# TensorE in program order for the first gate and up block of the feed-forward net

## The chip, the cores and the metric

The kernel runs on one core of a Trainium2 chip. The metric is the device time of one execution in microseconds; the kernel before takes 871.7 us (median of 3 runs, 871.03 to 872.21). Engines are named PE (TensorE, the matrix unit), DVE (VectorE), ACT (ScalarE), POOL (GpSimd) and SP (SyncE, which here issues nearly all DMAs). Each engine has its own queue of instructions and works it off in order; engines wait for one another through semaphores.

## What is computed

One layer of a decoder trunk for 512 tokens of width 1024 (float32): an input projection, sliding-window attention and gated linear attention side by side, a gated merge, a SwiGLU feed-forward net, a per-layer embedding gate and a last norm. The change touches the start of the feed-forward net:

```python
h = rms_norm(x, norm_ffn)
g, u = jnp.split(h @ w_ffn_in, 2, axis=-1)      # 1024 -> 2 x 2816
x = x + (jax.nn.silu(g) * u) @ w_ffn_out
```

## The kernel before

Matrix products in float32 accuracy are made of three products of split operands (`mm3`, L122 to L124): each operand is a high part (a copy, ACT, L111) and a low part (a subtraction, DVE, L112).

A gate or up block of 256 columns (`quad_pair`, L544) is computed by a Strassen-like scheme with seven products of quarter blocks instead of eight. In the names, fg00 is the first gate block, fu00 the first up block, fg01 the next gate block. Each block has four weight units (.0 to .3) and three PSUM banks (pa, pb, pc). One of the seven products is 12 matmuls (4 steps of `mm3`) of 128x256. In program order a block is: pa from unit .0; pb from .0; pa again from .1, accumulated on top; pc from .1; pa from .2; pb (other half) from .2; pa from .3. Since pa is a running sum, ACT copies it out after each of its products (`copy`, L580: fg00u twice, then fg00v, then g), and DVE adds such a copy to pb or pc (L576). The next product into pa may only start when the copy of the last has been made. The copies land in tiles of a pool with 8 buffers ("t2").

Ahead of the block stands the norm of x. Its rows are transposed, and the quarter blocks and the four Strassen sums of the activations are made by ACT and DVE (`column`, L1144; the names h2t, h_b, h_t). Between the transposes PE multiplies p by W_ple (pl0, pl1). ACT copies those results out (L1235, pl00o to pl13o, in t2 tiles too), and `aside` stores them to DRAM (L311) on SP's queue, behind the weight load issued last.

The order on each engine is made by a scheduler that goes by its own estimate of times, except inside a `manual_schedule` block, where the engines listed keep the order in which the code is written. In the kernel before, ACT, DVE and POOL keep the written order from behind the first up block on (L1306); PE is placed by the scheduler throughout the feed-forward net. For fg00 and fu00 the scheduler places all four engines.

Of the kernel before, what the change touches and what calls it, by code (L numbers as in the profile page):

```python
# [33 lines left out]
def hybrid_layer(  # L34
# [26 lines left out]
    nc = tc.nc  # L61
# [24 lines left out]
    def t2(name, shape=(P, 512), dt=F32):  # L86
        return tp.tile(list(shape), dt, tag="t2", name=name)
# [20 lines left out]
    def split(dst, src, scale=None, eng=nc.vector):  # L108
        hi, lo = dst
        if scale is None:  # L110
            ins = nc.scalar.copy(hi, src)  # L111
            eng.tensor_tensor(out=lo, in0=src, in1=hi.bitcast(F32), op=ALU.subtract)  # L112
        else:
            ins = nc.scalar.activation(hi, src, AF.Copy, scale=scale)  # L114
            nc.vector.scalar_tensor_tensor(  # L115
                out=lo, in0=src, scalar=scale, in1=hi.bitcast(F32), op0=ALU.mult, op1=ALU.subtract
            )
        return ins.ins
# [398 lines left out]
    def tok_inner(name, lhs, k0, nk, ncol, evac, per=2):  # L517

        nu = nk // per
        pss = [bank(f"{name}ps{t}") for t in range(NT)]  # L520
        for u in range(nu):
            w = W.take(f"{name}{u}")
            for t in range(NT):
                tok_mms(pss[t], w, lhs, t, k0 + per * u, per, ncol, u == 0, u == nu - 1)
                if u == nu - 1:
                    evac(t, pss[t])
                if t % 2:
                    yield
# [20 lines left out]
    def flush(late, every=False):  # L549

        for job in late or []:
            job[0] -= 1
        while late and (every or min(late)[0] < 1):
            late.pop(late.index(min(late)))[2]()
# [72 lines left out]
    def drive(stream, other=None, rate=1):  # L627
        for _ in stream:
            if other is not None:
                for _ in range(rate):  # L630
                    next(other, None)
# [533 lines left out]
    def xrow(t):  # L1165
        return xr[t // 2][:, t % 2, :]
# [84 lines left out]
    def x_half(i):  # L1251
        for t in (0, 1, 2, 3):
            ps = bank(f"xt{i}{t}")
            for j in range(4):
                nc.tensor.transpose(out=ps[:, tok(j)], in_=xrow(t)[:, tok(4 * i + j)], identity=ident)
            split(xT.part(i, ALL, tok(t)), ps.rearrange("p (j t) -> p j t", j=4))
            ss = sm.tile([P, 1], F32, tag="s2", name=f"x{i}{t}s")
            nc.scalar.activation(junk, xrow(t)[:, 512 * i : 512 * i + 512], AF.Square, accum_out=ss)
            if i == 0:
                part[t] = cpool.tile([P, 1], F32, name=f"x3{t}")  # L1260
                nc.vector.tensor_scalar(out=part[t], in0=ss, scalar1=4.0 / D, scalar2=4.0 * EPS, op0=ALU.mult, op1=ALU.add)
            else:
                m = add_mean(ss, D / 4, part[t], f"x{i}{t}m")
                r3[t] = cpool.tile([P, 1], F32, name=f"r3{t}")
                nc.gpsimd.tensor_tensor(out=r3[t], in0=m, in1=mhalf, op=ALU.pow)
            yield

    for gi, (f0, nf) in enumerate(FFN):
        act = Split(f"act{gi}", nf)

        def inner():
            for i in range(nf // 2):
                gs = [t2(f"g{gi}{i}{e}") for e in range(2)]
                us = []

                def silu(e, gs=gs):
                    yield [1, next(jobs), lambda: nc.scalar.activation(gs[e], gs[e], AF.Silu)]

                def mult(e, i=i, gs=gs, us=us):
                    yield [  # L1280
                        1 + e,
                        next(jobs),
                        lambda: nc.vector.tensor_tensor(out=us[e], in0=us[e], in1=gs[e], op=ALU.mult),  # L1283
                    ]
                    yield [3, next(jobs), lambda: split(act.rows(2 * i + e), us[e])]

                yield from quad_pair(f"fg{gi}{i}", h2.hT, gs, silu, late)
                us += [t2(f"u{gi}{i}{e}") for e in range(2)]
                yield from quad_pair(f"fu{gi}{i}", h2.hT, us, mult, late)

        def add_x2(i):
            def evac(t, ps):
                dst = xrow(t)[:, 512 * i : 512 * i + 512]
                nc.vector.tensor_tensor(out=dst, in0=ps, in1=dst, op=ALU.add)

            return evac

        stream, late, jobs = inner(), [], count()
        if gi == 0:
            for _ in range(8):  # L1300
                next(stream)

            W.after, W.SUMS = None, 4
            in_turn = tc.manual_schedule(engines={nc.scalar.engine, nc.vector.engine, nc.gpsimd.engine})
            in_turn.__enter__()
        drive(stream)  # L1306
        flush(late, True)
        drive(tok_inner(f"fo{gi}0", act, 0, nf, 512, add_x2(0)))
        last_half = tok_inner(f"fo{gi}1", act, 0, nf, 512, add_x2(1))
        if gi < len(FFN) - 1:  # L1310
            drive(last_half)
        else:
            in_turn.__exit__(None, None, None)
            drive(last_half, x_half(0), 1)
# [101 lines left out]
```

## Time and profile before

| | |
|---|---|
| median of 3 runs | 871.7 us |
| profiled execution, own time | 872.2 us |
| its span, first to last instruction | 870.4 us |
| PE busy | 854.0 us, 98% |
| DVE busy | 565.7 us, 65% |
| ACT busy | 446.2 us, 51% |
| POOL busy | 160.8 us, 18% |
| mean granted PE clock | 0.998 |

The span is the time between the first and the last instruction on the chip; the execution's own time is 1.8 us longer. Busy times are shares of the span and overlap between engines. A matmul's record is longer than its share of a stream, since matmuls are pipelined: the pace is read from start to start. Line numbers (L580) are those of the kernel before. In a timeline, a bracket at the end of a row gives the engine's idle time ahead of it and what ended it.

### The profile page before, as it was taken

The page shows a single profiled execution, that of the slowest core. Times are in us where ns is not written, and L with a number is a line of the kernel's source. Part 1 is how long each engine was busy: PE and PEld are TensorE (multiplying, and loading weights), DVE is VectorE, ACT ScalarE, POOL GpSimd, SP SyncE. Part 2 cuts the span into 40 slices and gives each one's busy share as a digit, 9 for nine tenths or more (in the row PEclk, how much of TensorE's full clock was granted, in tenths as well). Part 3 has the DMA queues.
Part 4 walks back from the last instruction along what each step waited for, and adds up shares of the span by engine and source line. Part 5 has one row for each costly group of instructions (what it writes and reads, how often), then busy time and mean ns, then how long its engine had stood idle before and what let it go on. Part 6 is the DMA issues. An engine that isn't in the chain of part 4 may idle for free. (4 is left out here: it accounts for less than half of the span.)

```text
span 870.4 us, 14739 instructions
## 1 busy us (share of the span) xinstructions
PE 854.0 (98%) x5901; PEld 748.7 (86%) x5901; DVE 565.7 (65%) x821; ACT 446.2 (51%) x859; POOL 160.8 (18%) x149
## 2 busy tenths in 40 slices
PE   8999989999999999999999999999999999999996
PEld 7977878888777788888887999889999889998886
DVE  5533866769876643356368799635998437985574
ACT  6336587866755543333256556413565314554453
POOL 4340434120221110100011222011232012210101
PEclk9999999999999999999999999999999999999999
DMA  9382423133764256774415233611316311422502
GB/s 282 103 215 78 152 74 97 50 102 102 236 206 158 74 170 216 271 265 146 142 54 164 94 126 108 232 49 49 95 52 211 129 49 49 136 87 94 194 1 98
DMA packets 88245, 113.29 MB, mean 130 GB/s; under 512 B 6152, under 2 KB 64304, under 8 KB 87792
## 3 DMA queue, kind: packets, MB, share of 16 engines
q1 hardware_dynamic: 86704, 107.43, 38.2%
q0 software_dynamic: 1456, 4.92, 1.6%
q8 instruction: 46, 0.75, 0.4%
q14 instruction: 23, 0.19, 0.1%
q10 hardware_dynamic: 16, 0.00, 0.0%
HBM read 95.35 MB, written 15.93 MB: 128 GB/s over the span
## 5 line engine op out<-in xcount | busy, mean ns | idle before, releaser
L111 ACT CAST fo_h<-raw 128x1024 fp32r<-128x1024 f32 x22 | 22.5, 1050 | 30.5 <-PE fo00ps L124 13.1
L112 DVE TENSOR_TENSOR fo_l<-raw,fo_h 128x1024 fp32r<-128x1024 f32 x22 | 26.3, 1220 | 12.1 <-ACT fo_h L111 12.1
L326 POOL TENSOR_TENSOR or<-om,mhalf 128x1 f32<-128x1 f32 x16 | 14.2, 886 | 68.1 <-DVE om L330 54.2
L112 DVE TENSOR_TENSOR act_l<-u,act_h 128x512 fp32r<-128x512 f32 x22 | 22.1, 1004 | 5.4 <-ACT act_h L111 5.4
L905 DVE TENSOR_TENSOR zs<-zs,kq 128x512 f32<-128x512 f32 x28 | 19.5, 707 | 7.0 <-ACT zs L901 6.3
L112 DVE TENSOR_TENSOR pg_l<-raw,pg_h 128x1024 fp32r<-128x1024 f32 x8 | 9.8, 1223 | 18.5 <-ACT pg_h L111 18.5
L112 DVE TENSOR_TENSOR wo_l<-raw,wo_h 128x1024 fp32r<-128x1024 f32 x8 | 9.8, 1224 | 17.7 <-ACT wo_h L111 17.7
L115 DVE SCALAR_TENSOR_TENSOR gt_l<-raw,gple,gt_h 128x256 fp32r<-128x256 f32 (+1 forms) x24 | 12.9, 570 | 12.0 <-ACT gt_h L114 11.9
L114 ACT ACTIVATE gt_h<-raw,gple 128x256 fp32r<-128x256 f32 (+1 forms) x24 | 12.6, 573 | 12.4 <-PE gt0ps L124 8.1
L111 ACT CAST act_h<-u 128x512 fp32r<-128x512 f32 x22 | 13.7, 622 | 10.0 <-DVE u L1283 10.0
L111 ACT CAST wo_h<-raw 128x1024 fp32r<-128x1024 f32 x8 | 8.4, 1053 | 20.1 <-PE wo0ps L124 6.6
L112 DVE TENSOR_TENSOR gg_l<-raw,gg_h 128x1024 fp32r<-128x1024 f32 x8 | 9.8, 1224 | 12.9 <-ACT gg_h L111 12.9
L899 DVE TENSOR_TENSOR zs<-G 128x512 f32<-128x512 f32 x24 | 16.1, 692 | 2.4 <-DMA G<-Gd 2.4
L111 ACT CAST pg_h<-raw 128x1024 fp32r<-128x1024 f32 x8 | 8.4, 1055 | 15.7 <-PE gg3pb L123 5.8
L112 DVE TENSOR_TENSOR v_l<-raw,v_h 128x1024 fp32r<-128x1024 f32 (+1 forms) x8 | 9.3, 1167 | 11.1 <-ACT v_h L111 11.1
L997 ACT ACTIVATE own<-o,or 128x256 f32<-128x256 f32 x16 | 7.6, 475 | 17.1 <-POOL or L326 16.9
L1283 DVE TENSOR_TENSOR u<-u,g 128x512 f32<-128x512 f32 x22 | 16.1, 733 | 0.0
L111 ACT CAST v_h<-raw 128x1024 fp32r<-128x1024 f32 (+1 forms) x10 | 9.6, 973 | 11.9 <-PE v2ps L124 4.5
L792 ACT ACTIVATE s_all<-s_all,nm 128x256 f32<-128x256 f32 (+1 forms) x32 | 15.2, 480 | 0.7 <-DVE nm L789 0.7
L112 POOL TENSOR_TENSOR qa<-qa,qs 64x768 fp32r<-64x768 f32 x2 | 7.2, 3616 | 41.6 <-ACT qs L111 41.5
L111 ACT CAST gg_h<-raw 128x1024 fp32r<-128x1024 f32 x8 | 8.4, 1049 | 12.2 <-PE ga3pb L123 4.2
L112 DVE TENSOR_TENSOR qa_l<-raw,qa_h 128x512 fp32r<-128x512 f32 x8 | 5.5, 719 | 13.2 <-ACT qa_h L111 13.2
(2312 smaller groups left out, 3550.1 us busy)
## 6 DMA issues: line engine op xcount, KB each, us to landing
raw<-in_w_ffn_in SPq DMA_DIRECT2D x44, 512.0 KB, 4.7
raw<-in_w_in SPq DMA_DIRECT2D x39, 512.0 KB, 4.7
raw<-in_w_ffn_out SPq DMA_DIRECT2D x22, 512.0 KB, 4.8
raw<-in_w_proj_gla SPq DMA_DIRECT2D x8, 512.0 KB, 5.7
mg<-mgd SPq DMA_DIRECT2D x8, 512.0 KB, 7.0
raw<-in_w_out SPq DMA_DIRECT2D x8, 512.0 KB, 4.5
raw<-in_w_ple_gate SPq DMA_DIRECT2D x8, 512.0 KB, 4.3
raw<-in_w_in SPq DMA_DIRECT2D x8, 256.0 KB, 5.0
```

Source lines behind the costliest of these rows:

```text
L111: ins = nc.scalar.copy(hi, src)
L112: eng.tensor_tensor(out=lo, in0=src, in1=hi.bitcast(F32), op=ALU.subtract)
L114: ins = nc.scalar.activation(hi, src, AF.Copy, scale=scale)
L115: nc.vector.scalar_tensor_tensor(out=lo, in0=src, scalar=scale, in1=hi.bitcast(F32), op0=ALU.mult, op1=ALU.subtract)
L326: return r, nc.gpsimd.tensor_tensor(out=r, in0=a, in1=mhalf, op=ALU.pow)
L792: nc.scalar.activation(s[:, a, :], s[:, a, :], AF.Exp, bias=nm[:, a : a + 1], accum_out=su[:, a : a + 1])
L899: pe.tensor_tensor(out=z3, in0=g3, in1=g3[:, :, b - 1 : b].broadcast_to([P, nb, 2 * b]), op=ALU.subtract)
L905: nc.vector.tensor_tensor(out=d4, in0=d4, in1=kq_, op=ALU.mult)
L997: nc.scalar.activation(v_[:, c, :], po[:, 0:256], AF.Copy, scale=r)
L1283: lambda: nc.vector.tensor_tensor(out=us[e], in0=us[e], in1=gs[e], op=ALU.mult),
```

## The change

The eight steps of the generator that make fg00 and fu00 now run inside a `manual_schedule` block for PE alone. PE gets their matmuls in the order in which the code is written. The scheduler still places ACT, DVE, POOL and SP there, and it takes PE's new order into account. No instruction's shape changes; ACT's two copies into fg00u stand next to each other now.

```diff
         stream, late, jobs = inner(), [], count()
         if gi == 0:
-            for _ in range(8):
-                next(stream)
+
+            with tc.manual_schedule(engines={nc.tensor.engine}):
+                for _ in range(8):
+                    next(stream)
```

Below is PE's queue before, from the last matmul of the second product of fg00 on, one row for each run of like matmuls. The operand on the left of the comma is the activation quarter (h_b) or sum (h_t).

```order
L124 MATMUL fg00pb<-h_b_4367,fg00.0_l 128x256
L122 MATMUL fg00pc<-h_b_4368,fg00.1_h 128x256
...
L122 MATMUL fu00pa<-h_b_4366,fu00.0_h 128x256
...
L122 MATMUL fu00pb<-h_b_4367,fu00.0_h 128x256
...
L122 MATMUL fu00pc<-h_b_4368,fu00.1_h 128x256
...
L122 MATMUL fg00pa<-h_t_4370,fg00.1_h 128x256
...
L122 MATMUL fg00pb<-h_t_4369,fg00.2_h 128x256
```

And PE's queue at the same place now:

```order
L124 MATMUL fg00pb<-h_b_4367,fg00.0_l 128x256
L122 MATMUL fg00pa<-h_t_4370,fg00.1_h 128x256
...
L122 MATMUL fg00pc<-h_b_4368,fg00.1_h 128x256
...
L122 MATMUL fg00pa<-h_t_4371,fg00.2_h 128x256
...
L122 MATMUL fg00pb<-h_t_4369,fg00.2_h 128x256
...
L122 MATMUL fg00pa<-h_t_4372,fg00.3_h 128x256
...
L122 MATMUL fu00pa<-h_b_4366,fu00.0_h 128x256
```

The second product into pa stood behind three others and the head of a fourth; now it follows directly on the two products of unit .0. From the first matmul into fg01pb on, both queues are the same. On ACT the queue is unchanged up to the copy pl13o; behind it stood before:

```order
L1235 ACTIVATE pl12o<-pl1ps_4685 128x512
L1235 ACTIVATE pl13o<-pl1ps_4686 128x512
L111 CAST fu00.1_h<-fu00.0s_4688 128x1024
L580 COPY fg00u<-fg00pa 128x256
L111 CAST fu00.2_h<-fu00.0s_4687 128x1024
L580 COPY fg00u<-fg00pa 128x256
```

and now stands:

```order
L1235 ACTIVATE pl12o<-pl1ps_4685 128x512
L1235 ACTIVATE pl13o<-pl1ps_4686 128x512
L580 COPY fg00u<-fg00pa 128x256 x2
L111 CAST fu00.1_h<-fu00.0s_4688 128x1024
L580 COPY fg00v<-fg00pa 128x256
L111 CAST fu00.2_h<-fu00.0s_4687 128x1024
```

The first copy of pa moved one place forward, from behind the cast of fu00.1 to directly behind pl13o. DVE's queue differs in the same stretch only (its sums of pa and pb against the splits of fu00 and fg01), SP's and POOL's not at all.

## Rows read from the trace of the kernel before

**Rows 1.** Waits of PE, whole span: us in total, times, longest.

```profile
PE pt L806 <- ACT s_all L796: 2.4, 1, 2.4
...
PE fu00pc L122 <- ACT fu00.1_h L111: 1.1, 1, 1.1
PE fu00pa L124 <- DVE fu00.0_l L112: 1.0, 1, 1.0
```

**Rows 2.** Windows: length, PE, PEld, DVE, ACT, POOL busy (instructions), clock, DMA, GB/s.

```profile
467.97:493.96 25.99, 23.45 (x181) 22.02 (x180) 19.25 (x26) 15.39 (x26) 5.94 (x4) 1.00 0.36 122
...
500.00:600.00 100.00, 100.00 (x665) 92.49 (x664) 69.23 (x81) 43.09 (x67) 15.30 (x11) 1.00 0.34 114
```

**Rows 3.** Timeline of PE, 467 to 496 us: start, duration, engine, line, what.

```profile
467.97 0.28 PE L122 MATMUL fg00pa<-h_b,fg00.0_h 128*128 128x256 f32 x1
...
469.40 0.28 PE L122 MATMUL fg00pb<-h_b,fg00.0_h 128*128 128x256 f32 x1
...
470.72 0.28 PE L124 MATMUL fg00pb<-h_b,fg00.0_l 128*128 128x256 f32 x1
...
486.17 0.39 PE L122 MATMUL fu00pa<-h_t,fu00.1_h 128*128 128x256 f32 x1 [0.42 <-ACT fu00u L580]
...
493.96 0.28 PE L122 MATMUL fg01pb<-h_b,fg01.0_h 128*128 128x256 f32 x1
...
495.40 0.28 PE L122 MATMUL fg01pa<-h_t,fg01.1_h 128*128 128x256 f32 x1
```

**Rows 4.** Timeline of ACT, 475 to 486 us.

```profile
475.09 0.60 ACT L1235 ACTIVATE pl13o<-pl1ps 128x512 f32<-128x512 f32 x1
476.78 1.04 ACT L111 CAST fu00.1_h<-fu00.0s 128x1024 fp32r<-128x1024 f32 x1 [1.09 <-PE fu00pb L123]
477.73 0.37 ACT L580 COPY fg00u<-fg00pa 128x256 f32<-128x256 f32 x1
...
485.74 0.38 ACT L580 COPY fu00u<-fu00pa 128x256 f32<-128x256 f32 x1
```

**Rows 5.** Timeline of DVE, 471 to 475 us.

```profile
471.36 1.36 DVE L112 TENSOR_TENSOR fg00.3_l<-raw,fg00.3_h 128x512 fp32r<-128x512 f32 x1
...
474.38 0.68 DVE L112 TENSOR_TENSOR h_t<-h2t,h_t 128x512 fp32r<-128x512 f32 x1
```

**Rows 6.** Timeline of SP's queue, 472 to 474 us.

```profile
472.78 0.37 SPq L243 DMA_DIRECT2D raw<-in_w_ffn_in  x1
473.19 0.51 SPq L311 DMA_DIRECT2D pwd<-pl00o  x1
473.74 0.43 SPq L311 DMA_DIRECT2D pwd<-pl01o  x1
```

**Rows 7.** DMA issues, 450 to 500 us: count, KB each, us to landing.

```profile
pwd<-pl01o SPq DMA_DIRECT2D x1, 256.0 KB, 4.5
...
pwd<-pl10o SPq DMA_DIRECT2D x1, 256.0 KB, 4.4
```

**Rows 8.** Timeline of the span's end: PE's last matmul.

```profile
862.33 0.28 PE L124 MATMUL gt2ps<-gt_h,xT_l 128*128 128x256 f32 x1
```

**Rows 9.** Windows at the span's end, columns as in rows 2.

```profile
866.00:867.00 1.00, 0.00 (x0) 0.00 (x0) 0.55 (x1) 0.61 (x1) 0.14 (x1) 1.00 0.01 0
...
868.00:870.40 2.40, 0.00 (x0) 0.00 (x0) 0.00 (x0) 0.00 (x0) 0.00 (x0) 0.50 0.38 152
```

**Rows 10.** Timeline of PE, the first 16 us (x8 counts merged instructions).

```profile
1.46 1.46 PE L370 MATMUL idle<-ones 128*128 128x512 bf16 x3 [1.46 <-DVE ones L365]
...
6.56 1.89 PE L370 MATMUL idle<-ones 128*128 128x512 bf16 x4
8.24 1.92 PE L436 MATMUL n_0t<-ident,xn 128*128 128x128 f32 x8
...
11.00 0.34 PE L122 MATMUL v0ps<-v_h,h_h 128*128 128x400 f32 x1
...
15.00 1.04 PE L436 MATMUL n_1t<-ident,xn 128*128 128x128 f32 x8
```

## The prediction

> **What bounds the kernel now.** I read the page's busy shares first: PE 854.0 of 870.4 us, no other engine above 65%. Next the waits of PE [rows 1]: the longest in the whole kernel is 2.4 us, and two of about 1 us lie in the stretch of the change, fu00pc and fu00pa waiting for split weights. Then the windows [rows 2]: from 467.97 to 493.96 PE issues 181 matmuls, 180 of them ahead of the next block's pb; from 500 to 600 it is busy throughout, and the list of its waits has none behind this stretch. So whatever time this stretch gains or loses arrives unshortened at the end of the kernel: nothing later has slack that could take it up, and the work behind fg01pb keeps its order. The question is only when the first matmul into fg01pb starts. Before, that is 493.96 [rows 3].
>
> **What the change removes.** A product of 12 matmuls runs at 469.40 - 467.97 = 1.43 us, and one further on at 495.40 - 493.96 = 1.44 us [rows 3]; I take 1.435. Between 467.97 and 493.96 lie 15 products (14 of fg00 and fu00 and one of fg01): 15 x 1.435 = 21.5 us, against 25.99 us taken. So 4.5 us are bubbles, waits and small restarts. Program order can win back at most these 4.5 us.
>
> **What it adds.** The second product into pa must not start until ACT has copied the first out (L580). Before, PE had two whole products of fu00 and one of fg00 to do meanwhile; they now stand behind it. So PE stands still from its last matmul into fg00pb, which starts at 470.72 and ends at 471.00 [rows 3], until that copy is made. Queued behind the waiting matmul are all of the 13 products that remain up to fg01pb.
>
> When is the copy made? Two things hold it.
>
> First, ACT's queue. The copy stands behind pl13o in the new order as in the old. pl13o runs at 475.09 for 0.60 us [rows 4], and it can't move forward: it goes into a buffer that DVE frees with its last piece of the activations' Strassen sums, which ends at 474.38 + 0.68 = 475.06 [rows 5]. DVE's and ACT's queues up to there are unchanged, and nothing in them waits for a matmul that moves. So ACT is free at about 475.6. That DVE piece is also the last of the activation operands, so none of them is later than the copy.
>
> Second, the copy's target. fg00u is a t2 tile, and its buffer was last held by pl00o, whose store must have landed. That result was ready long before, but its store sits in SP's queue behind a weight load that waits for DVE's fg00.3_l (471.36 + 1.36 = 472.72): the load goes out at 472.78, the store at 473.19 [rows 5, 6]. The trace has no landing time for this one. Its neighbours land 4.4 and 4.5 us after issue [rows 7]; I take 4.4, so 477.6. From above it is bounded by the copy itself, which began at 477.73 in the kernel before [rows 4], directly behind the cast of fu00.1, so that this wait didn't show. From below, if the store lands much sooner than its neighbours, ACT's 475.6 decides.
>
> So the copy runs at 477.6, 0.37 us long [rows 4], and PE follows 0.05 us after its end (copy of fu00u 485.74 + 0.38 = 486.12, matmul at 486.17 [rows 3, 4]): PE resumes at 478.05. Bounds: 476.0 (475.6 + 0.37 + 0.05) and 478.15 (477.73 in place of 477.6). From there 13 products at 1.435 are 18.66 us, and I add 0.1 us for the restart: fg01pb starts at 496.8. **Term 1: 496.8 - 493.96 = +2.85 us** (bounds +0.8 and +2.95). All 4.5 us of bubbles are taken as gone in it. What hides the later copies: in program order each product into pa is followed by one into pb or pc, 1.435 us, over a copy of 0.37 us; and ACT's casts of fu00.1, fu00.2 and fu00.3, about 1.05 us each, fall in this time as well, with fu00's products five and more places behind the first copy. If that cover fails once, it costs some 0.5 to 1 us.
>
> **The clock.** PE would stand still for 478.05 - 471.00 = 7.05 us; its longest wait so far was 2.4. What such a gap does is seen in this trace only at its end: the last matmul ends at 862.33 + 0.28 = 862.61 [rows 8], the granted clock is still 1.00 over 866 to 867, and 0.50 behind 868, that is 1.2 instead of 2.4 GHz [rows 9]. So it fell between 4.4 and 5.4 us after PE went idle, sooner than 7.05. I therefore count on the lower level when PE resumes. How long it lasts I take from the kernel's start. There the clock column prints 1.00 throughout, so I go by durations: eight transposes took 1.92 us at 8.24 and 1.04 us at 15.00, a factor of 1.85; matmuls ran without a break from 6.56, and their starts are at the later spacing from 11.00 on, 4.4 us after [rows 10]. In 4.4 us at 1/1.85 of the pace PE falls behind by 4.4 x (1 - 1/1.85) = 2.0 us. **Term 2: +2.0 us.** Bounds: 0 if the clock stays, and 4.4 if the slow stretch is as long as from the kernel's first matmul, 1.46, to 11.00 (9.5 us x 0.46). The copies of ACT hide all the better while PE is slow.
>
> The Trainium skill ("TensorE: Matmul & The Clock Gate", section "Why this matters for your kernels") warns of long idle gaps between bursts of matmuls, since TensorE goes back to its lower clock after them; by that rule the term is there, without it the sum is term 1 alone. The same page (section "Terms") prices time at the lower level at one minus the ratio of clocks, which would make an estimate of 2.2 us of the 4.4 us. The end of this trace agrees with the first; of the second no run here yet shows a gap in the middle of a kernel.
>
> **The sum.** +2.85 + 2.0 = +4.85 us. On the profiled execution's own 872.2 us (span 870.4 and 1.8 around it) that is 877.05; it lies 0.5 above the median of 871.7. On the median: 876.5 us.
>
> **Rivals.**
> 1. The clock stays up through the gap. For it: the one fall seen came 4.4 to 5.4 us after the last matmul, and nothing says that a gap in the middle starts counting at its first moment. Against it: 7.05 is a good deal longer. Then term 1 alone: 871.7 + 2.85 = 874.5. Chance 0.14.
> 2. The slow stretch lasts as long as at the kernel's start from its first matmul, or a second wait appears in the new ACT order: term 2 up to 4.4, 871.7 + 2.85 + 4.4 = 878.9. For it: the activity ahead of 6.56 was thin, so 4.4 may be too short a reading of a process that began earlier. Against it: behind the gap come dense products. Chance 0.11.
> 3. The store lands early, and PE resumes at 476.0. The gap is 5.0 us, inside the bracket in which the clock fell, so it is open whether it does: 871.7 + 0.8 = 872.5 without, 874.5 with. For it: no landing time of pl00o is recorded. Against it: two neighbours with 4.4 and 4.5. Chance 0.05.
> 4. Faster: program order wins back the bubbles, because the copy is made before PE misses it. The price is up to -4.5 us (867.2), and the point from which it decides is a resumption before 493.96 - 18.75 = 475.2. For it: the two waits of about 1 us and the restarts are real and go away. Against it: pl13o alone holds ACT until 475.69, so that ACT would have to take the copy ahead of it, and the order doesn't. Chance 0.04.
> 5. That the change doesn't do what it says has no chance of its own: PE's queue shows the written order.
>
> **How the numbers follow.** The forecast, terms 1 and 2 together, has 0.66. Its own spread is about 875.5 to 877.5 (resumption 0.1 to 0.4 us either way, slow stretch 3 to 6 us). The range takes in rival 1 and half of rival 2: 874.0 to 878.6; left out are rivals 3 and 4 and the far half of 2, some 0.15. Differences under 0.2%, 1.7 us, can't be told from no change. Slower by more than that is above 873.4: the forecast, rivals 1 and 2 and part of 3, 0.92. Within: most of rival 3 without the clock and a weak form of 4, 0.05. Faster: 0.03.
>
> **What would show it.** In the changed kernel's profile: one wait of PE, fg00pa for ACT's fg00u, of about 7 us, at the head of the list; ACT's copy starting at 477.6, idle ahead of it, released by a DMA (pwd from pl00o); the window 471 to 482 with a granted clock below 1, and matmuls into fg00pa and fg00pc some 0.2 us apart where they were 0.12; no wait of PE over 0.5 us from there to fg01pb; and fg01pb at about 498.8 instead of 493.96, with the same distance kept at every later landmark. I am wrong if the copy starts at 475.6, if the clock reads 1.00 throughout, or if fg01pb comes before 496.

## The result and the profile after

The changed kernel takes 876.36 us (median of 4 runs, 875.62 to 877.16), the kernel before 871.44 us (4 runs, 871.03 to 872.21). The ratio is 1.0051, its 95% interval 1.0038 to 1.0064: slower by about half a per cent, 4.92 us between the medians. The forecast was 876.5 us, from a sum of +4.85 us. The four runs fall into two pairs (877.16 and 877.04; 875.68 and 875.62), so the median lies between two levels that both occur; the profiled execution is the 877.16, for which the forecast on its own base was 877.05.

The waits of PE over the whole span of the changed kernel, to be set beside [rows 1] (us in total, times, longest):

```profile
PE fg00pa L122 <- ACT fg00u L580: 7.1, 1, 7.1
...
PE pt L806 <- ACT s_all L796: 1.8, 1, 1.8
```

The two waits for split weights, fu00pc and fu00pa, are gone; a single one of 7.1 us stands at the head. The timeline of PE there answers to [rows 3]:

```profile
468.43 0.28 PE L122 MATMUL fg00pa<-h_b,fg00.0_h 128*128 128x256 f32 x1
...
471.18 0.28 PE L124 MATMUL fg00pb<-h_b,fg00.0_l 128*128 128x256 f32 x1
478.51 0.58 PE L122 MATMUL fg00pa<-h_t,fg00.1_h 128*128 128x256 f32 x1 [7.05 <-ACT fg00u L580]
478.89 0.42 PE L123 MATMUL fg00pa<-h_t,fg00.1_h 128*128 128x256 f32 x1
479.11 0.42 PE L124 MATMUL fg00pa<-h_t,fg00.1_l 128*128 128x256 f32 x1
...
482.74 0.40 PE L123 MATMUL fg00pc<-h_b,fg00.1_h 128*128 128x256 f32 x1
482.95 0.31 PE L124 MATMUL fg00pc<-h_b,fg00.1_l 128*128 128x256 f32 x1
483.10 0.28 PE L122 MATMUL fg00pc<-h_b,fg00.1_h 128*128 128x256 f32 x1
483.21 0.28 PE L123 MATMUL fg00pc<-h_b,fg00.1_h 128*128 128x256 f32 x1
...
499.29 0.28 PE L122 MATMUL fg01pb<-h_b,fg01.0_h 128*128 128x256 f32 x1
```

Read it from start to start. Up to 471.18 and from 483.10 on, matmuls begin 0.12 us apart; from 478.89 to 482.74, 18 steps take 3.85 us, 0.214 us each. The whole stretch, first matmul into fg00pa to first into fg01pb, lasts 499.29 - 468.43 = 30.86 us against 25.99 before [rows 3]: +4.87. That is the loss that the change makes: the shift found at fg01pb (5.33 us on the time axis, 0.46 of it already there at 468.43) stays to PE's last matmul, which starts at 867.65, 5.32 us behind [rows 8]. The 0.46 us arise ahead of the change, in part at a stretch of lower clock near 114 us, which the last section shows; whole times contain it, the stretch doesn't.

The timeline of ACT, which holds the copy (to [rows 4]):

```profile
475.53 0.60 ACT L1235 ACTIVATE pl13o<-pl1ps 128x512 f32<-128x512 f32 x1
478.09 0.37 ACT L580 COPY fg00u<-fg00pa 128x256 f32<-128x256 f32 x1 [1.96 <-DMA pwd<-pl00o]
481.48 0.37 ACT L580 COPY fg00u<-fg00pa 128x256 f32<-128x256 f32 x1 [3.02 <-PE fg00pa L124]
```

and SP's queue, which issued the store it waits for (to [rows 6]):

```profile
473.22 0.37 SPq L243 DMA_DIRECT2D raw<-in_w_ffn_in  x1
473.63 0.51 SPq L311 DMA_DIRECT2D pwd<-pl00o  x1
```

ACT was free at 476.13 and stood idle for 1.96 us more, released by a DMA: the store of pl00o, issued at 473.63 and done by 478.09, 4.46 us later. PE follows 0.05 us behind the copy. Last, the windows of that stretch (columns as in [rows 2]; the granted clock is the third number from the right):

```profile
475.00:476.00 1.00, 0.00 (x0) 0.00 (x0) 0.49 (x1) 0.99 (x2) 0.00 (x0) 1.00 0.83 253
476.00:477.00 1.00, 0.00 (x0) 0.00 (x0) 0.00 (x0) 0.12 (x1) 0.00 (x0) 0.58 1.05 365
477.00:478.00 1.00, 0.00 (x0) 0.00 (x0) 0.00 (x0) 0.00 (x0) 0.00 (x0) 0.50 1.05 403
...
482.00:483.00 1.00, 1.00 (x7) 1.00 (x7) 0.00 (x0) 0.00 (x0) 0.00 (x0) 0.51 0.92 233
483.00:484.00 1.00, 1.00 (x10) 1.00 (x10) 0.29 (x1) 0.41 (x1) 0.00 (x0) 1.00 0.79 265
```

PE's last matmul ended at 471.46. The clock reads 1.00 until 476, falls to 0.50 soon after (0.58 over 476 to 477 puts the fall at 476.16, 4.7 us after that end), 1.2 in place of 2.4 GHz, and is back at about 483, some 4.5 us after PE took up work at 478.51.

### The profile page after: what moved, and what is told of

Its sections match the earlier page's. It is cut to its first block, busy times and chain, and to the rows that moved or that the text cites. A ratio compares the mean times of both kernels' runs of the same rounds, so it can differ in the third digit from the quotient of the medians.

```text
span 875.4 us, 14733 instructions
## 1 busy us (share of the span) xinstructions
PE 856.0 (98%) x5901; PEld 752.2 (86%) x5901; DVE 569.5 (65%) x821; ACT 446.4 (51%) x859; POOL 158.7 (18%) x149
## 3 DMA queue, kind: packets, MB, share of 16 engines
q0 software_dynamic: 1456, 4.92, 1.6%
## 5 line engine op out<-in xcount | busy, mean ns | idle before, releaser
L111 ACT CAST fo_h<-raw 128x1024 fp32r<-128x1024 f32 x22 | 22.5, 1050 | 30.5 <-PE fo10ps L124 13.1
L1277 ACT ACTIVATE g<-g 128x512 f32<-128x512 f32 x22 | 14.0, 634 | 0.1
```

## The experiments

The theory is the prediction's: the loss is the copy's wait for a store that landed late, plus the pace at the lower clock that the gap brings. Rivals: that ACT's queue alone (pl13o) holds the copy and the store is beside the point; that the clock reading goes with the gap but costs little; and that the loss comes from program order as such, wherever it is applied. Each median stands beside the kernel before on the same chip: 871.75 us (29 runs) in the first set, which holds fill48, store_early, store_early_fill and up_only, 871.79 us (17 runs) in the second; the changed kernel belongs to neither and has the 871.44 us (4 runs) of the first section beside it. "Stretch" is first matmul into fg00pa to first into fg01pb, in the profiled run. The mean clock is that of the whole profiled run; it takes in what happens near 114 us (last section) and behind the last matmul, so it doesn't tell by itself what the clock did in the stretch. The medians follow the stretch, beside the kernel before, to within 0.9 us.

| kernel | median us (runs) | ratio, 95% interval | stretch us | mean clock |
|---|---|---|---|---|
| before | 871.75 / 871.79 | 1 | 25.99 | 0.998 |
| changed | 876.36 (4) | 1.0051, 1.0038 to 1.0064 | 30.86 | 0.992 |
| fill48 | 877.22 (6) | 1.0058, 1.0044 to 1.0071 | 31.17 | 0.998 |
| store_early | 872.67 (11) | 1.0014, 1.0005 to 1.0023 | 27.61 | 0.996 |
| store_early_fill | 872.01 (11) | 1.0001, 0.9992 to 1.0009 | 26.13 | 0.998 |
| up_only | 872.63 (11) | 1.0010, 1.0001 to 1.0018 | 26.93 | 0.995 |
| fill12 | 874.24 (7) | 1.0027, 1.0016 to 1.0038 | 28.71 | 0.997 |
| own_sched | 869.34 (11) | 0.9978, 0.9968 to 0.9987 | 23.96 | 0.995 |
| own_early_order | 869.26 (5) | 0.9965, 0.9953 to 0.9978 | 23.24 | 0.996 |
| own_early_sched | 867.14 (5) | 0.9949, 0.9937 to 0.9962 | 22.23 | 0.997 |

### fill48: dummy matmuls in the gap, to keep the clock up

In the changed kernel, behind the first add of fg00; their result is overwritten:

```diff
         add(c[0][:, H[0]], pb[:, H[0]], p1)
+        if name == "fg00":
+            hi, _ = act.q("b11")
+            for j in range(48):
+                nc.tensor.matmul(pc[:, H[1]], lhsT=hi[:, j % 4, 0:P], rhs=hi[:, j % 4, :], start=True, stop=True)
```

> The changed kernel, with 48 dummy matmuls (128x256, into the half of the bank pc that fg00 doesn't use) in TensorE's queue between the second product and the one that waits for the copy; ACT's, DVE's, POOL's and SP's queues stay as in the changed kernel. They end about 1.2 us before the copy. My theory (wait 2.85 us and lower clock 2.0 us): the clock stays at 1.00 through the gap, the copy comes no later, and 2.0 us come back: 874.3 us (871.4 + 2.9), fg01pb 2.0 us earlier than in the changed kernel. Rival (the whole loss is the wait, and the lower clock is hidden by other waits): no change, 876.4 us. Rival (the clock falls whatever lies in the gap): 876.4 us with a granted clock of 0.5 behind the gap.

It took 877.22 us: no gain at all. Its windows show that the clock did stay up:

```profile
476.00:478.00 2.00, 1.06 (x9) 0.85 (x8) 0.00 (x0) 0.00 (x0) 0.00 (x0) 1.00 1.05 394
478.00:480.00 2.00, 0.00 (x0) 0.00 (x0) 0.00 (x0) 0.00 (x0) 0.00 (x0) 1.00 1.04 395
```

but its ACT made the copy at 480.01, though ACT reached pl13o at 475.19, 7.11 us after the stretch's first matmul, as in the changed kernel (7.10):

```profile
480.01 0.37 ACT L580 COPY fg00u<-fg00pa 128x256 f32<-128x256 f32 x1 [4.22 <-DMA pwd<-pl00o]
```

The wait for the store grew from 1.96 to 4.22 us, which ate what the clock gave. Its DMA issues (count, KB, us to landing) say that all these stores landed late, not this one alone:

```profile
pwd<-pl01o SPq DMA_DIRECT2D x1, 256.0 KB, 6.8
pwd<-pl02o SPq DMA_DIRECT2D x1, 256.0 KB, 6.9
pwd<-pl03o SPq DMA_DIRECT2D x1, 256.0 KB, 7.2
```

In the changed kernel these three took 4.6, 4.7 and 4.8. The experiment changed a second thing with the first and could not tell the clock's share; it did show how directly that landing time sets the end. Its runs, 875.1 to 878.6, scatter more than those of the kernel before.

### fill12: the same with a quarter of the instructions

A plain float32 matmul keeps PE busy longer (in the trace 12 of them take 5.42 us, 0.45 each; 32 of the short ones take 4.07 in store_early_fill), so 12 of them cover the gap:

```diff
+        if name == "fg00":
+            hi = act.q("b11")[0].bitcast(F32)
+            for j in range(12):
+                nc.tensor.matmul(pc[:, H[1]], lhsT=hi[:, j % 4, 0:P], rhs=hi[:, j % 4, :], start=True, stop=True)
```

> The changed kernel again with a filled gap, now with 12 dummy matmuls in float32 (128x256, four passes each, some 5 us together) in place of 48 short ones: a quarter of the added instructions. In fill48 the stores of pl00o to pl12o landed 6.2 to 7.2 us after issue instead of 4.1 to 4.8, in the same stretch as a 16 KB code load of 0.95 us at 477.5 (in the changed kernel at 483.9), and the copy came at 480.0 with the clock up. My theory: the code load that the 96 added instructions moved forward was what delayed the stores; here it stays behind them, the copy comes 9.7 us after the first matmul of fg00 as in the changed kernel, the clock stays at 1.00, and the first matmul into fg01pb comes 28.9 us after the first into fg00pa (30.9 in the changed kernel, 26.0 before): 874.3 us. Rival (a busy TensorE itself delays the stores): copy 11.9 us after the first matmul, 877 us, as in fill48. Rival (the lower clock costs nothing): 30.9 us, 876.4 us.

As expected: 874.24 us, stretch 28.71. The windows show a clock of 1.00 throughout from 470 to 480; three of them:

```profile
474.00:476.00 2.00, 1.20 (x6) 0.72 (x4) 0.00 (x0) 0.46 (x1) 0.00 (x0) 1.00 1.00 347
476.00:477.00 1.00, 0.33 (x2) 0.33 (x3) 0.01 (x1) 0.37 (x1) 0.00 (x0) 1.00 1.05 406
477.00:478.00 1.00, 1.00 (x11) 1.00 (x10) 0.42 (x1) 0.00 (x0) 0.00 (x0) 1.00 1.06 410
```

ACT's copy waits for pl00o as in the changed kernel, and comes 9.48 us after the stretch's first matmul (9.66 there):

```profile
476.25 0.37 ACT L580 COPY fg00u<-fg00pa 128x256 f32<-128x256 f32 x1 [1.78 <-DMA pwd<-pl00o]
```

The stores land as they did there (pl01o 4.4 us after issue). At 476 to 477 PE is idle for part of the time and the clock holds; from 477 matmuls run 10 or 11 to the microsecond at once, where the changed kernel had 7 after its gap. So the fall of the clock was taken away, and the stretch became 30.86 - 28.71 = 2.15 us shorter. Of these, 0.18 us are the copy, which came that much earlier; about 2.0 us are the clock. The medians differ by 876.36 - 874.24 = 2.1 us, or by 4.92 - 2.45 = 2.5 us when each is set against the kernel before in its own set. What is left over the kernel before, 28.71 - 25.99 = 2.72 us, is the wait alone.

### store_early: the stores ahead of the weight load

The stores of the p rows go out where they are written in p_proj, and not over the helper that delays them; in SP's queue the first four, pl00o to pl03o, move ahead of three transfers of weights (in the changed kernel the last of these goes out at 473.22, just ahead of pl00o); on the other engines nothing changes its place:

```diff
-                aside(pwd[t, :, 512 * i : 512 * i + 512], o)
+                nc.sync.dma_start(pwd[t, :, 512 * i : 512 * i + 512], o)
```

> The changed kernel, with the stores of pl00o to pl13o no longer tied to follow the weight load issued last; TensorE's, ACT's, DVE's and POOL's queues stay as in the changed kernel, only SP's differs. My theory (the copy fg00u waits for the store of pl00o to land, and without that for ACT to finish pl13o): the copy starts at about 476.0 on the time axis of the changed kernel's profile instead of 478.09, TensorE resumes at 476.45, the gap is 5.0 us instead of 7.05. That lies just where the clock fell before (4.96 us after the last matmul), so 872.3 us if it stays, 874.3 if it falls, runs of both kinds possible. Rival (the store is not what holds the copy; ACT's queue or the sums of DVE are): copy at 478, 876.4 us.

872.67 us, stretch 27.61. ACT's timeline:

```profile
473.25 0.61 ACT L1235 ACTIVATE pl13o<-pl1ps 128x512 f32<-128x512 f32 x1
473.73 0.39 ACT L580 COPY fg00u<-fg00pa 128x256 f32<-128x256 f32 x1
```

No idle time stands in front of the copy now: the wait for the store is gone and pl13o alone holds it. That tells the store from ACT's queue, and both count: the queue sets the lower bound, the store what came on top. The edit moved a second thing. In the changed kernel pl13o began at 475.53, when DVE's last piece of the sums was done; here it begins together with that piece. The first row is the changed kernel's, the second store_early's:

```profile
474.81 0.68 DVE L112 TENSOR_TENSOR h_t<-h2t,h_t 128x512 fp32r<-128x512 f32 x1
473.25 0.68 DVE L112 TENSOR_TENSOR h_t<-h2t,h_t 128x512 fp32r<-128x512 f32 x1
```

So with early stores pl13o no longer waits for the buffer that this piece frees, and PE's gap is 4.28 us where 5.0 were expected. The windows show what it did to the clock:

```profile
472.00:474.00 2.00, 0.00 (x0) 0.00 (x0) 1.92 (x3) 2.00 (x5) 0.00 (x0) 1.00 0.61 129
474.00:476.00 2.00, 1.83 (x10) 1.83 (x11) 0.42 (x1) 0.12 (x1) 0.00 (x0) 0.66 0.99 354
476.00:477.00 1.00, 1.00 (x7) 1.00 (x7) 0.00 (x0) 0.24 (x1) 0.00 (x0) 0.50 1.05 402
477.00:478.00 1.00, 1.00 (x6) 1.00 (x6) 0.00 (x0) 0.14 (x1) 0.00 (x0) 0.50 1.06 271
478.00:479.00 1.00, 1.00 (x11) 1.00 (x10) 0.11 (x1) 0.23 (x1) 0.00 (x0) 0.97 1.03 324
```

PE works again from 474.17, and the clock still falls behind that point, to be back at about 478: 0.66 over 474 to 476 puts the fall at 474.6, 4.7 us after the end of the last matmul, as in the changed kernel (the expectation's 4.96 is nearer to a count from its start). The shorter gaps at this place did not lower it: 3.38 us in fill48, 1.47 in fill12.

### store_early_fill: both terms away

store_early with 32 of the dummy matmuls of fill48.

> Early stores as in store_early, and 32 dummy matmuls in the gap as in fill48 (3.8 us, so that they end before the copy). My theory: what is left is the bound of a copy behind pl13o, +0.8 us on the kernel before, with the clock at 1.00: 872.2 us. Rival (program order itself costs time further on, in fu00): more than 873 us. Rival (the store doesn't matter): the same as fill48.

872.01 us, the interval includes no change; stretch 26.13, 0.14 us over before. PE's wait is down to a quarter of a microsecond:

```profile
474.89 0.39 PE L122 MATMUL fg00pa<-h_t,fg00.1_h 128*128 128x256 f32 x1 [0.24 <-ACT fg00u L580]
```

PE resumes 7.31 us after the stretch's first matmul here and in store_early alike, so the 27.61 - 26.13 = 1.48 us between the two stretches are the clock alone, for 3.4 us at the lower level. The medians are only 0.66 us apart.

With both terms gone the loss is gone, and program order with early stores is level with the kernel before; early stores alone under the scheduler's order were not run. It does not win either: what it saves in bubbles goes into the wait for the copy behind pl13o, which the dummies fill. The prediction's lower bound for the wait was +0.8 us; it came to 0.14 because pl13o itself moved forward with the early stores, to 6.39 us after the stretch's first matmul in store_early and in this kernel, from 7.10 in the changed one.

### up_only: program order for the up block alone

```diff
+            for _ in range(4):
+                next(stream)
             with tc.manual_schedule(engines={nc.tensor.engine}):
-                for _ in range(8):
+                for _ in range(4):
                     next(stream)
```

> Only the up block fu00 is held in program order on TensorE; the gate block fg00 is placed by the scheduler. (Program order for the gate block alone gives, instruction by instruction, the queues of the changed kernel.) In the queue, two products of fu00 and one of fg00 stand again behind the first two. My theory (the loss is made by the gate block's second product into pa standing directly behind its first two): the gap is about 1.2 us, the clock stays at 1.00, but the products of fu00 that filled later waits are now behind fg00, so that some 0.8 us of waits for the copies into fu00u and fg00v come instead: 872.2 us, 871 to 873. Rival (program order as such costs, in either block): 873.9 us, half of the change's loss. Rival (program order in the up block wins back the bubbles): 870.1 us.

872.63 us, stretch 26.93. The gate block alone in program order gives the queues of the changed kernel instruction for instruction, so the changed kernel stands for it: +4.87 us in the stretch, and +0.94 for the up block alone. Its waits of PE in the stretch are four small ones:

```profile
PE fg00pa L122 <- ACT fg00u L580: 1.3, 1, 1.3
PE fu00pa L124 <- DVE fu00.0_l L112: 1.0, 1, 1.0
PE fu00pa L122 <- ACT fu00u L580: 0.8, 1, 0.8
PE fg00pa L122 <- ACT fg00v L580: 0.7, 1, 0.7
```

The loss is not spread over program order; it hangs on what stands ahead of the second product of fg00.

### own_early_order, own_early_sched, own_sched: the first copy made early

If the copy's wait is the cause, the copy should be given a buffer of its own, with nothing to wait for but PE's product:

```diff
+        if name == "fg00":
+            p1 = wp.tile([P, 256], F32, tag="own", name="fg00w", bufs=1)
         run = pa[:, H[0]]
```

own_early_order has this and the early stores in the changed kernel; own_early_sched the same two edits in the kernel before, whose order is the scheduler's; own_sched the buffer alone in the kernel before.

> The changed kernel (fg00 and fu00 in program order) with early stores, and with a buffer of its own for the first copy of fg00pa, so that ACT takes that copy before it casts fu00.0, ahead of the four copies of pl1. My theory (program order loses only through the late first copy): TensorE runs on into the second product into pa and the one into pc, and then waits some 1.5 us for the second copy, which still stands behind pl13o; 11 products remain. First matmul of fg00pa to first of fg01pb: 23.2 us instead of 26.0 before, 868.7 us, clock at 1.00. Rival (the sums of the activations are late as well, t3 and t4 after pl13o): another 1 us, 869.7. Rival (program order loses for another reason): 871.5 or more.

> The kernel before (TensorE placed by the scheduler) with early stores and the own buffer for the first copy of fg00pa. The scheduler then places the second product into pa and the one into pc directly behind the first two, and one product of fu00 in the wait that follows. My theory (bubbles are won back by an early copy, not by the order): 22 to 22.5 us from the first matmul of fg00pa to the first of fg01pb, 867.7 us, below both kernels and below own_early_order. Rival (program order is better once the copy is early): above own_early_order.

> The kernel before with the own buffer for the first copy of fg00pa only; the stores stay late. The scheduler fills the wait for the second copy (its buffer waits for the store of pl01o, landed at about 478.3) with two products of fu00 and most of a third. My theory: the 1 us waits go, the second copy comes at 478.3 and delays TensorE by some 0.5 us: about 22.5 us in the stretch, 868.2 us. Rival (late stores cost the same wherever the first copy goes): 26 us, 871.5 us.

own_early_order: 869.26 us, stretch 23.24; the stretch is as expected (23.2), the median 0.56 us above the expected 868.7. The first copy follows PE at once, and the next wait is for the second copy, which now stands behind pl13o in its turn. First ACT:

```profile
469.97 0.37 ACT L580 COPY fg00w<-fg00pa 128x256 f32<-128x256 f32 x1 [0.64 <-PE fg00pa L124]
474.73 0.60 ACT L1237 ACTIVATE pl13o<-pl1ps 128x512 f32<-128x512 f32 x1
475.21 0.39 ACT L580 COPY fg00u<-fg00pa 128x256 f32<-128x256 f32 x1
```

and then PE, whose 1.40 us are all that is left of the gap:

```profile
475.65 0.38 PE L122 MATMUL fg00pa<-h_t,fg00.2_h 128*128 128x256 f32 x1 [1.40 <-ACT fg00u L580]
```

own_early_sched: 867.14 us, the best of all: 4.65 us below the kernel before (ratio and interval in the table) and some 9 us below the changed kernel. Its stretch is 22.23 us, and the one wait of PE left in it is

```profile
474.44 0.39 PE L122 MATMUL fg00pb<-h_t,fg00.2_h 128*128 128x256 f32 x1 [0.20 <-DVE g L576]
```

So 3.8 of the 4.5 us that the prediction called bubbles can be won, by freeing the copy and not by the order: with both edits, program order is 2.1 us slower than the scheduler's (869.26 against 867.14; 1.0 us in the stretch).

own_sched missed: 869.34 us and a stretch of 23.96, where 868.2 and about 22.5 were expected. Without the early stores the second copy waits for the next store in the same way:

```profile
478.90 0.37 ACT L580 COPY fg00u<-fg00pa 128x256 f32<-128x256 f32 x1 [1.56 <-DMA pwd<-pl01o]
```

and PE stands 1.35 us for it. Five of its stores took 5.2 to 5.8 us (pl01o 5.6), where 4.6 had been reckoned with, from the changed kernel. PE's wait explains 0.85 us of the 1.5 that the stretch is longer than expected; the rest stays open.

## Why the prediction was right

- **What the change removes.** All 4.5 us of bubbles were taken as gone. From the end of the copy to fg01pb it holds: 499.29 - 478.51 = 20.78 us, of which 13 products at 1.435 are 18.66; the 2.12 us left are the clock (2.0) and next to no bubble. No second wait appeared, so the cover of the later copies held.
- **The copy and its store (term 1, +2.85).** Landing was taken as 4.4 us and was 4.46. On a time axis that runs 0.46 us later from before the stretch, the copy was due at 477.6 + 0.46 = 478.06 and came at 478.09, PE at 478.51 for 478.51. fill12 measures the term by itself: +2.72 in the stretch. The store's part is shown by store_early, where the copy follows pl13o without a wait. That pl13o can't move forward held in the changed kernel, but not with early stores, so +0.8 us is no lower bound of program order as such.
- **The clock (term 2, +2.0).** The fall came 4.7 us after the end of the last matmul, inside the bracket of 4.4 to 5.4 read from the span's end [rows 9]. The slow pace lasted 4.5 us, where 4.4 was read from the kernel's start [rows 10]. A matmul takes 0.214 us in place of 0.12 in it, so it costs 4.5 x (1 - 0.12 / 0.214) = 2.0 us; fill12 gives about 2.0 by taking it away, and the same sum for store_early's 3.4 us makes 1.5, where 1.48 were measured. The Trainium skill ("TensorE: Matmul & The Clock Gate", section "Why this matters for your kernels") warns of just such a gap, and the gaps of 7.05 and 4.28 us agree. The price that the Trainium skill gives in the section "Terms" of the same page, one minus the ratio of clocks, would make 2.25 us of the 4.5 as an estimate; the measured step of 0.214 to 0.12, a factor of 1.79, puts it a little lower.
- **The shift arrives whole.** It does: no wait behind the stretch took any of it up. From the first matmul into fg01pb to the end of the span it is 376.0 to 376.1 us in the changed kernel and in all eight experiments (changed kernel: 875.4 - 499.29; own_early_sched: 865.3 - 489.19), 376.4 in the kernel before. That own_early_sched gains 3.76 us in the stretch and 4.65 in the medians is therefore not made behind the stretch.
- **Rivals.** In the changed kernel's profile the clock did not stay up and the store was not early. Program order as such gained nothing: level with the kernel before at best (store_early_fill, which had early stores besides), and behind the scheduler's order where both had the early copy.
- **What is luck.** The median sits between two pairs of runs 1.4 us apart, and only one of the upper pair has a profile. The lower pair has a higher mean clock, 0.994 against 0.992; 0.002 of 875 us is 1.75 us of full clock, or 3.5 us at half. That fits a run without the low stretch near 114 us as well as one with a shorter low stretch behind the gap, and which it is was not shown. That the profiled pair differs by 877.16 - 872.21 = 4.95 us, so near to the stretch's 4.87, is luck too: 0.46 us from ahead of the stretch and some 0.4 the other way behind fg01pb all but cancel. The expectation for store_early had reckoned with its gap lying at the edge. Its runs spread from 872.0 to 874.6 us, but those of the kernel before beside it spread as far, from 870.6 to 873.0, so that their spread shows nothing.

## What to carry to other kernels

Before an order is written out by hand, look for what the first instruction that it makes the engine wait for is itself waiting for: here a copy's target buffer, held by a store that sat behind a weight load in another queue. The gaps of PE of 4.28 and 7.05 us cost twice in these runs, once as a wait and again as matmuls at the lower clock, while one of 3.38 us cost once; the length of a gap alone does not tell, as the next section shows. A buffer of its own for one 128x256 copy and an earlier store were worth 4.65 us (3.76 in the stretch), and program order nothing.

## What the runs showed of the hardware that was not expected

- The clock can fall after work has been taken up again: in store_early PE stood still for 4.28 us from 469.9 and worked from 474.17, and yet the window 476 to 477 has a granted clock of 0.50. It was back at about 478, some 4 us after the resumption, as in the changed kernel (4.5).
- The same short gap can lower the clock in one execution and not in another. Some 350 us ahead of the change, where no edit reaches, PE stands still for 1.84 us and then does the same work in the changed kernel and in fill12. Behind it the clock falls in the first and stays up in the second (each a row of PE's timeline, then the window 114 to 118):

```profile
113.53 0.62 PE L806 MATMUL pt<-ident,s_all 128*128 128x128 f32 x2 [1.84 <-ACT s_all L796]
114.00:118.00 4.00, 4.00 (x20) 3.74 (x20) 1.21 (x3) 3.76 (x15) 3.25 (x3) 0.57 0.00 0
...
113.43 0.62 PE L810 MATMUL pt<-ident,s_all 128*128 128x128 f32 x2 [1.84 <-ACT s_all L800]
114.00:118.00 4.00, 3.54 (x28) 3.17 (x27) 1.11 (x3) 3.76 (x14) 3.38 (x3) 1.00 0.00 0
```

The window reads 0.62 to 0.65 in up_only, own_sched and own_early_order, and 1.00 in the other six profiles, the kernel before among them, where PE stood still for 2.42 us. It costs 0.94 us: from the first matmul into pt to the first into pov it is 119.00 - 113.53 = 5.47 us in the changed kernel and 117.96 - 113.43 = 4.53 in fill12. So part of the scatter of whole times arises ahead of every edit.

- The landing time of the same 256 KB stores went from 4.1 to 4.8 us (changed kernel) to 5.4 to 7.2 (fill48, all six that have one). Keeping PE busy is not the reason, since fill12 did so and kept 4.1 to 5.2. In fill48 a load of instruction code lies among the stores, at 477.54; in own_sched, with 5.2 to 5.8 us for five of its stores, there is one at 476.52. In the changed kernel it comes at 483.94, behind the landing of all these stores. fill12 has one at 479.1, and only the last two of its stores took 5.2 us. In own_sched the two stores issued behind the load took 4.1 and 4.3 us. That the added instructions move these code loads, and that the loads delay the stores, fits these times but was not tested by itself.

The queues of fill48's DMAs from 474 to 480 us (packets, MB, share) show that load as the one packet beside the data:

```profile
q1 hardware_dynamic: 1300, 1.96, 94.0%
q8 instruction: 1, 0.02, 1.0%
```

With a share of 1.0% it takes little room itself, so a delay of 2 us and more would have to come about in another way than by the bytes it moves; that stays open.
